# Gate and up products from seven half products, a feed-forward in two halves, adaLN weights in lots of four

## Chip, cores and metric

The kernel runs on one core of one Trainium2 chip. The metric is the device time of one execution in microseconds (us). TensorE (PE) multiplies, VectorE (DVE), ScalarE (ACT) and GpSimd (POOL) work elementwise, SyncE (SP) issues the loads. Before the change the median of three runs is 2294.38 us.

## What is computed

One inference step of a trunk of two layers, for a prompt of 512 tokens and 8 sequences with one new token each, 520 columns in all. Every layer has a feed-forward, a token mixer (gated delta rule beside windowed attention) and a second feed-forward. Each of them normalises its input, scales and shifts it by vectors made from a conditioning vector (adaLN), and adds its gated result to the residual stream. All in float32. The part that the change is about:

```python
def _adaln(c, w_ada, b_ada):
    m = jax.nn.silu(c) @ w_ada + b_ada
    return m.reshape(c.shape[0], N_MOD, 1, D_MODEL)      # 9 vectors of 1024

def _modulate(x, g, shift, scale):
    return _rms_norm(x, g) * (1.0 + scale) + shift

def _swiglu(h, w_gu, w_down):                            # w_gu (1024, 2 * 2816), w_down (2816, 1024)
    a, b = jnp.split(h @ w_gu, 2, axis=-1)
    return (jax.nn.silu(a) * b) @ w_down

def _layer(x, c, pos, conv_buf, S0, k_buf, v_buf, prm):
    ...
    m = _adaln(c, w_ada, b_ada)
    h = _modulate(x, g_ffn1, m[:, 0], m[:, 1])
    x = x + 0.5 * m[:, 2] * _swiglu(h, w_ffn1_gu, w_ffn1_down)
    h = _modulate(x, g_mix, m[:, 3], m[:, 4])
    ...
    x = x + m[:, 5] * mix
    h = _modulate(x, g_ffn2, m[:, 6], m[:, 7])
    x = x + 0.5 * m[:, 8] * _swiglu(h, w_ffn2_gu, w_ffn2_down)
```

## The kernel before

The residual stream `x` stays in SBUF with the 1024 features in 8 blocks of 128 partitions and the 520 tokens as columns. The columns are cut in two halves, a = 0 (256 columns) and a = 1 (264: 256 of the prompt and the 8 new tokens). Every product has a weight block of 128 by 128 as the stationary operand and up to 264 token columns as the moving one.

Float32 accuracy comes from three passes in a faster format: each operand is split into a rounded part and a rest (`whi` and `wlo` of the weights, `hh` and `hl` of the normalised input, `ghi` and `glo` of the gated values), and hh by whi, hl by whi and hh by wlo are summed in PSUM. `mmk` writes these three matmuls for one feature block k and one half, `mmk2` for both halves.

The class `Stream` (`W`) brings the weights: a `raw` tile of 1024 columns is loaded, cut in pieces of 512 columns (four blocks k), and each piece is split by one ACT copy (`whi`) and one DVE subtraction (`wlo`), into rings of eight buffers. `take` hands the next piece to the products; `advance` splits as many pieces ahead as the ring has room for, and is called after every block k.

A feed-forward (`ffn`) has 22 tiles of 128 hidden features. A tile needs a gate and an up product (`product`, 8 blocks k, 2 halves, 3 matmuls: 48 matmuls each), then `gate`: Silu on ACT, a product on DVE, and the split into `ghi` and `glo`. Tiles 0 and 1 are made by `head`, which goes over half a = 0 first, while half a = 1 is still being normalised by DVE and ACT (`Norm.apply`, one block k after the other; `norm.need` sets how far it must be). After the 22 tiles come 8 down products (22 blocks k each), whose results are added to `x` (`xupdate`); the last two of them are done half by half in `tail`, so that the normalisation of the next sub-layer can begin on half 0 while PE still works on half 1.

Work that is not in this line (the adaLN vectors, and most of the mixer) is in generators in a list (`Fill`). After every block k `fill.step` asks a clock model of the kernel's own whether a generator's next piece is ready, and writes its instructions there. `ada_gen` is one of these: for one adaLN vector it loads two groups of 8 weight tiles of 256 KB, and writes their 16 matmuls one after the other; four column groups of PE work on four of them at a time. Buffers for all this (`slot`) come from one pool of 48.

The stretch of the trace that is spoken of below, in order: feed-forward 1 of layer 0 to about 465 us, its mixer to about 777 us, feed-forward 2 of layer 0 to about 1198, feed-forward 1 of layer 1 to about 1595, the mixer, and feed-forward 2 of layer 1 from about 1907 us.

Of the kernel before, what the change touches and what calls it, by code (L numbers as in the profile page):

```python
# [25 lines left out]
SLOTS = 48  # L26
# [64 lines left out]
class Fill:  # L91
# [50 lines left out]

    def force(self):
# [15 lines left out]
class Stream:  # L159
# [3 lines left out]
    def __init__(self, ops, raw_p, hl_p, n_raw, n_sub):  # L163
        self.ops, self.raw_p, self.hl_p, self.n_raw, self.n_sub = ops, raw_p, hl_p, n_raw, n_sub
        self.descs, self.raw, self.subs = [], {}, []
        self.nd = 0
        self.free_raw = 0
        self.todo = []
        self.late = None
        self.out = 0  # L170

    def add(self, ap, keep=None):

        self.descs.append(ap)
        n = ap.shape[1]
        for o in range(0, n, 512):
            self.subs.append((len(self.descs) - 1, o, min(512, n - o), o + 512 >= n, keep))

    def advance(self, done, must=-1):
# [3 lines left out]
        while True:  # L183
# [9 lines left out]
            j = len(self.todo)  # L193
            if j < len(self.subs) and self.subs[j][0] < self.nd and self.room(done, j) and (
                    j <= must or clk.ready([self.raw[self.subs[j][0]]]) < clk.pe + 1.0):
                d, o, n, last, keep = self.subs[j]
                raw = self.raw[d]
# [14 lines left out]

    def rest(self):

        if self.late:
            j, d, lo, raw, hi = self.late
            self.late = None
            self.ops.tt(out=lo, in0=raw, in1=hi, op=ALU.subtract)
            if d is not None:
                del self.raw[d]  # L220
                self.free_raw = d + 1
# [17 lines left out]
class Ops:  # L239
# [22 lines left out]
    def mm(self, out, lhsT, rhs, start, stop, frac=1.0):  # L262
        self.nc.tensor.matmul(out, lhsT=lhsT, rhs=rhs, start=start, stop=stop)  # L263
# [73 lines left out]
def trunk(ctx, tc, xT, cT, cst, rope, vec, gu1, dn1, win, wba, wout, gu2, dn2, ada,  # L337
# [5 lines left out]
    raw_p = ctx.enter_context(tc.tile_pool(name="rawp", bufs=3))  # L343
# [8 lines left out]
    W = Stream(ops, raw_p, hl_p, 3, 8)  # L352

# [38 lines left out]
    hh = [(small(f"hh{a}", (128, KD, HALF[a][1]), F32R), small(f"hl{a}", (128, KD, HALF[a][1]), F32R)) for a in range(2)]  # L392
# [7 lines left out]
    def ada_load(l, g):  # L400
        t = []
        for k in range(KD):
# [5 lines left out]
    def ada_mm(t, pa, u=0, first=True, last=True):  # L408


        for k in range(KD):
            r = k % 4
            mm(pa[32 * r:32 * r + 32], lhsT=sc[:, u, k, :], rhs=t[k], start=first and k < 4, stop=last and k >= 4, frac=0.27)
# [17 lines left out]
    room = [True]  # L431
    mod_done = {(0, 0), (0, 1)}

    def ada_gen(l0):

        def load():
            if room[0] and mods and mods[0][0] <= l0:
                l, j = mods.pop(0)
                return l, j, ada_load(l, 2 * j), ada_load(l, 2 * j + 1)

        nxt = load()
        while nxt:
            l, j, t0, t1 = nxt
            yield t1
            pa = aux()
            ada_mm(t0, pa, 0, True, False)
            ada_mm(t1, pa, 1, False, True)
            m_sb = ada_out(pa)
            nxt = load()
            yield m_sb,  # L450
            ada_turn(l, 2 * j, m_sb, None, 2)
            mod_done.add((l, j))
# [87 lines left out]
    def mmk(out, w, k, src, kk, a, first, last, M=128):  # L540

        wh, wl = w
        for wi, (wt_, part) in enumerate(((wh, 0), (wh, 1), (wl, 0))):
            mm(out, lhsT=wt_[:, k * M:(k + 1) * M], rhs=src(a, part, kk), start=first and wi == 0, stop=last and wi == 2)
# [8 lines left out]
    def h_src(a, part, k):  # L553
        return hh[a][part][:, k, :]
# [24 lines left out]
    def head(norm):  # L579
# [18 lines left out]
        for k in range(KD):  # L598
            norm.need(1, k)
            for i in range(4):  # L600
                mmk(banks[1][i], ws[(k // 4) * 4 + i], k % 4, h_src, k, 1, k == 0, k == KD - 1)
            if k == 3:
# [81 lines left out]
    def ffn(l, j, norm, nxt, last, first=head):  # L684
        ghi, glo = [], []

        def gate(pg, pu):
# [7 lines left out]
            hi, lo = slot("ghi", F32R), slot("glo", F32R)  # L695
            act(out=hi, in_=t, func=AF.Copy)
            tt(out=lo, in0=t, in1=hi.bitcast(F32), op=ALU.subtract)
            ghi.append(hi)
            glo.append(lo)

        b = first(norm)
        gate(b[0], b[1])
        gate(b[2], b[3])
        for f in range(2, FF):
            room[0] = f < 12
            pg = product(h_src)
            pu = product(h_src)
            gate(pg, pu)

        def g_src(a, part, k):  # L710
            o, n = HALF[a]
            return (ghi, glo)[part][k][:, o:o + n]

        nrm = nxt() if nxt else None
        ops.table(EXP)
        for m in range(KD - 2):
            p = product(g_src, FF)
            for a in range(2):
                xupdate(l, j, m, p[a], a)
                if nrm is not None:  # L720
                    nrm.square(m, a)
            if last:
# [1042 lines left out]
```

## Time before, and how to read its profile

| what | value |
|---|---|
| median of three runs | 2294.38 us (2291.13 to 2298.29) |
| the profiled execution | 2294.32 us, of it 2292.5 us of span |
| PE busy | 2230.0 us (97%), 18154 matmuls |
| DVE busy | 1084.5 us (47%), 2586 instructions |
| ACT busy | 866.2 us (38%), 1861 instructions |
| POOL busy | 76.5 us (3%), 73 instructions |

Busy times are sums over the instructions of an engine. A matmul's own time in the trace (280 to 290 ns) is longer than the spacing at which matmuls follow each other (about 120 ns), since they overlap in the array; what a matmul costs is read from the spacing, that is from a stretch of the chain divided by its count. The same holds in a small way for DVE.

### The profile page before, as it was taken

The numbers are of one execution on the slowest core, as the hardware profiler recorded it, in microseconds if no ns is written. First come the engines' busy times: TensorE is split into PE (matmuls) and PEld (weight loads), VectorE is DVE, ScalarE is ACT, GpSimd is POOL, SyncE is SP. The second block draws the span as 40 slices with busy tenths as digits, with TensorE's granted clock in tenths as the row PEclk, the third lists the DMA queues.
The fourth block names the chain that finished last, engine by engine and source line by source line (L and its number), as shares of the span: only waits on it lengthen the run. The fifth ranks groups of instructions, "written<-read, shape, count | busy, mean of one in ns | idle before, by whom it ended". The sixth has DMA issues, their size and how long they took to land.

```text
span 2292.5 us, 43781 instructions
## 1 busy us (share of the span) xinstructions
PE 2230.0 (97%) x18154; PEld 2118.9 (92%) x18154; DVE 1084.5 (47%) x2586; ACT 866.2 (38%) x1861; POOL 76.5 (3%) x73
## 2 busy tenths in 40 slices
PE   7999999999988999999999999999998989999999
PEld 5879999989977988999999999999997879999999
DVE  5323333476787733333345333335687776333332
ACT  4323332356744422233234333323646444333321
POOL 0000000000121000000000000000001200000000
PEclk8999999999999999999999999999999999999999
DMA  8894223243224499422322222233432233222331
GB/s 270 317 325 148 93 86 95 91 96 104 84 66 130 170 326 337 155 93 86 95 88 93 93 92 93 85 95 101 88 103 63 77 134 120 92 89 89 94 113 52
DMA packets 172918, 287.75 MB, mean 126 GB/s; under 512 B 49936, under 2 KB 87472, under 8 KB 172720
## 3 DMA queue, kind: packets, MB, share of 16 engines
q1 hardware_dynamic: 172720, 284.96, 38.6%
q8 instruction: 142, 2.33, 0.4%
q14 instruction: 56, 0.46, 0.1%
HBM read 271.55 MB, written 14.41 MB: 125 GB/s over the span
## 4 chain that ended last, share of the span: by engine, by line
PE 85%; DVE 6%; issue 5%; ACT 3%; DMA 1%; POOL 0%; SPq 0%; DVEq 0%; POOLq 0%
PE acc L263 68%; PE aux L263 15%; DVE wlo L298 1%; DVE s L298 1%; PE aux L273 1%; ACT sq L290 1%; DVE hl L298 0%; DVE t L298 0%; DVE vr L298 0%; DVE w L298 0%; ACT whi L290 0%; POOL swa L307 0%; DVE ss L298 0%; DVE sq L298 0%; DVE x L298 0%
## 5 line engine op out<-in xcount | busy, mean ns | idle before, releaser
L263 PE MATMUL acc<-hh,whi 128*128 128x256 f32 x3440 | 742.1, 290 | 19.0 <-DVE x L298 12.3
L263 PE MATMUL acc<-hh,wlo 128*128 128x256 f32 x3440 | 721.1, 284 | 1.2 <-DVE wlo L298 1.2
L263 PE MATMUL acc<-hl,whi 128*128 128x256 f32 x3440 | 721.6, 284 | 0.0
L290 ACT ACTIVATE whi<-raw 128x512 fp32r<-128x512 f32 (+1 forms) x672 | 406.1, 617 | 751.4 <-PE acc L263 621.7
L298 DVE TENSOR_TENSOR wlo<-raw,whi 128x512 fp32r<-128x512 f32 (+1 forms) x672 | 437.4, 681 | 377.6 <-ACT whi L290 377.5
L263 PEld LDWEIGHTS acc<-hh,whi 128*128 128x128 f32 x3440 | 548.2, 189 | 58.0 <-issue 32.8
L263 PEld LDWEIGHTS acc<-hh,wlo 128*128 128x128 f32 x3440 | 546.1, 189 | 2.6 <-DVE wlo L298 2.6
L263 PEld LDWEIGHTS acc<-hl,whi 128*128 128x128 f32 x3440 | 547.3, 189 | 0.2
L263 PE MATMUL acc<-ghi,wlo 128*128 128x256 f32 x1232 | 262.0, 282 | 0.0
L263 PE MATMUL acc<-glo,whi 128*128 128x256 f32 x1232 | 261.7, 282 | 0.0
L263 PE MATMUL acc<-ghi,whi 128*128 128x256 f32 x1232 | 261.7, 282 | 0.0
L298 DVE TENSOR_TENSOR g<-g,acc 128x256 f32<-128x256 f32 (+1 forms) x168 | 64.2, 422 | 342.6 <-PE acc L263 306.0
L263 PEld LDWEIGHTS acc<-ghi,whi 128*128 128x128 f32 x1232 | 196.8, 188 | 0.0
L263 PEld LDWEIGHTS acc<-ghi,wlo 128*128 128x128 f32 x1232 | 196.6, 188 | 0.0
L263 PEld LDWEIGHTS acc<-glo,whi 128*128 128x128 f32 x1232 | 196.6, 188 | 0.0
L290 ACT ACTIVATE ghi<-g 128x520 fp32r<-128x520 f32 x88 | 56.2, 639 | 218.5 <-DVE g L298 218.5
L298 DVE SCALAR_TENSOR_TENSOR x<-acc,mt,x 128x256 f32<-128x256 f32 x72 | 33.6, 480 | 141.8 <-PE acc L263 141.8
L298 DVE TENSOR_TENSOR glo<-g,ghi 128x520 fp32r<-128x520 f32 x88 | 61.6, 701 | 62.2 <-ACT ghi L290 62.2
L263 PE MATMUL aux<-hl,whi 128*128 128x264 f32 x304 | 86.7, 285 | 0.8 <-DVE hl L298 0.8
L263 PE MATMUL aux<-hh,whi 128*128 128x264 f32 x304 | 86.9, 286 | 0.0
L263 PE MATMUL aux<-hh,wlo 128*128 128x264 f32 x304 | 86.4, 284 | 0.0
L263 PE MATMUL aux<-ada,sc 128*32 128x512 f32 (+1 forms) x640 | 71.6, 575 | 6.5 <-DMA ada<-in_ada 6.5
(289 smaller groups left out, 2145.1 us busy)
## 6 DMA issues: line engine op xcount, KB each, us to landing
raw<-in_gu SPq DMA_DIRECT2D x176, 512.0 KB, 3.2
ada<-in_ada SPq DMA_DIRECT2D x288, 256.0 KB, 5.4
raw<-in_dn SPq DMA_DIRECT2D x64, 512.0 KB, 3.5
raw<-in_win SPq DMA_DIRECT2D x44, 512.0 KB, 3.3
raw<-in_dn SPq DMA_DIRECT2D x32, 384.0 KB, 3.2
raw<-in_wout SPq DMA_DIRECT2D x22, 512.0 KB, 3.5
s<-in_s SPq DMA_DIRECT2D x16, 256.0 KB, 4.4
bv<-vnd SPq DMA_DIRECT2D x16, 256.0 KB, 4.3
```

The costliest lines, as they stand in the source:

```text
L263: self.nc.tensor.matmul(out, lhsT=lhsT, rhs=rhs, start=start, stop=stop)
L273: self.nc.tensor.transpose(out, in_, ident)
L290: self.nc.scalar.activation(**k)
L298: getattr(self.nc.vector, f)(**k)
```

## The change

The first matrix, h by the gate and up columns, is cut in two by two blocks: the tokens into the two halves a, the 1024 features into blocks k 0 to 3 and 4 to 7, and the columns of a tile into gate and up. The eight block products of a tile are replaced by seven (Strassen's scheme, in Winograd's form), for 78 of the 88 tiles: tiles 0 and 1 of each feed-forward, and in the first one tiles 2 and 3 too (`FIRST`), stay as they were.

- `add_pair` and `add_up`: for each such tile four sums of weight pieces are made on POOL (`sum`, 512 columns), and seven pieces are split in place of four.
- `combine`: once for a feed-forward, for each of four pairs of blocks k, POOL adds `hl` to `hh` again (four adds of 264 columns), DVE makes the four sums of the scheme from that (`y`), and ACT and DVE split them into four tiles `th`.
- `seven`: seven products of four blocks k, 12 matmuls each, five of them over 264 columns and two over 256. Three of them write on top of what another product left in the same PSUM bank, after ACT has copied it out (`u`); DVE adds the copies.
- The feed-forward is done in two halves of 11 tiles (`PARTS`), each followed by its 8 down products over 11 blocks k, so `x` is updated twice as often and each item of `tail` has 11 blocks k.
- `ada_gen` loads and multiplies lots of four tiles, four lots for an adaLN vector, as far as slots are free (`fits`), and writes them into PSUM buffers of the kind `acc` while the seven products run.
- 51 slots in place of 48, four `raw` tiles in place of three; `hh` and `hl` of half 0 are padded with zeros to 264 columns.

```diff
+    def add_pair(self, a0, a1):
+        d0, d1 = len(self.descs), len(self.descs) + 1
+        self.descs += [a0, a1]
+        a11, a12, a21, a22 = (("raw", d, o) for d in (d0, d1) for o in (0, 512))
+        j = len(self.subs)
+        s1, s2, s3, s4 = (("sum", j + i) for i in (3, 2, 4, 5))
+        self.sums += [(j + 2, s1, a21, a22, ALU.add, d1), (j + 2, s2, s1, a11, ALU.subtract, d1),
+                      (j + 4, s3, a11, a21, ALU.subtract, d1), (j + 5, s4, a12, s2, ALU.subtract, d1)]
+        self.uses.update({s1: 2, s2: 2, s3: 1, s4: 1})
+        for q in (a11, a12, s2, s1, s3, s4, a22):
+            self.subs.append((d1, q, 512, d1 if q == a22 else None, None))
...
+            t = self.made[q] = self.new_sum()
+            self.ops.pool("tensor_tensor", out=t, in0=self.source(x), in1=self.source(y), op=op)
...
-    def ada_mm(t, pa, u=0, first=True, last=True):
-        for k in range(KD):
-            r = k % 4
-            mm(pa[32 * r:32 * r + 32], lhsT=sc[:, u, k, :], rhs=t[k], start=first and k < 4, stop=last and k >= 4, frac=0.27)
+    def ada_mm(t, pa, u, h):
+        for r in range(4):
+            mm(pa[32 * r:32 * r + 32], lhsT=sc[:, u, 4 * h + r, :], rhs=t[r], start=u + h == 0, stop=u + h == 2, frac=0.27)
+        drop(*t)
...
+    def combine(norm, th):
+        for k in range(4):
+            yield lambda: norm.done[1] >= k + 5
+            h1, h2 = (slot("h32", F32, (128, 2, 264)) for _ in range(2))
+            for t, kk in ((h1, k), (h2, k + 4)):
+                for a in range(2):
+                    pool("tensor_tensor", out=t[:, a], in0=hh[a][0][:, kk, :].bitcast(F32),
+                         in1=hh[a][1][:, kk, :].bitcast(F32), op=ALU.add)
+            yield h1, h2
+            y0, y1 = (slot("y", F32, (128, 2, 264)) for _ in range(2))
+            tt(out=y0[:, 0], in0=h1[:, 1], in1=h1[:, 0], op=ALU.subtract)
+            tt(out=y1[:, 0], in0=h2[:, 1], in1=h1[:, 1], op=ALU.subtract)
+            tt(out=y0[:, 1], in0=h2[:, 1], in1=y0[:, 0], op=ALU.subtract)
+            tt(out=y1[:, 1], in0=h2[:, 0], in1=y0[:, 1], op=ALU.subtract)
...
+            act(out=x[0], in_=y0, func=AF.Copy)
+            act(out=x[2], in_=y1, func=AF.Copy)
+            yield y0, y1
+            tt(out=x[1], in0=y0, in1=x[0].bitcast(F32), op=ALU.subtract)
+            tt(out=x[3], in0=y1, in1=x[2].bitcast(F32), op=ALU.subtract)
...
+        def seven():
...
+            prod(pb, 264, of_h(0, 0, 264), True)
+            act(out=u1[:, 0], in_=pb[:, 0:264], func=AF.Copy)
+            prod(pa, 256, of_h(0, 4, 256), True)
+            tt(out=t0, in0=pa[:, 0:256], in1=u1[:, 0, 0:256], op=ALU.add)
+            prod(pb, 264, of_t(0, 1), False)
+            act(out=u1[:, 1], in_=pb[:, 0:264], func=AF.Copy)
+            act(out=t0, in_=t0, func=AF.Silu)
+            prod(pc, 264, of_t(0, 0), True)
+            act(out=u2[:, 1], in_=pc[:, 0:264], func=AF.Copy)
+            prod(pb, 264, of_t(2, 0), False)
+            act(out=u2[:, 0], in_=pb[:, 0:264], func=AF.Copy)
+            prod(pc, 264, of_h(1, 4, 264), False)
+            tt(out=t1, in0=pc[:, 0:264], in1=u1[:, 1], op=ALU.add)
+            tt(out=u2[:, 1], in0=u2[:, 1], in1=u2[:, 0], op=ALU.add)
+            prod(pb, 256, of_t(2, 1, 256), False)
...
+        for part, (f0, f1) in enumerate(PARTS):
+            nk = f1 - f0
+            for f in range(max(f0, 2), f1):
...
+                fill.until(lambda: len(th) == 4)
+                pairs[0] = True
+                seven()
```

What the change does to the order of the instructions, at three places.

DVE, the instructions of one tile in the middle of a feed-forward, and the first of the next, before (`g` is the gated tile, `acc` its PSUM):

```order
L298 TENSOR_TENSOR wlo<-raw,whi 128x512 x4
L298 TENSOR_TENSOR g<-g,acc 128x256
L298 TENSOR_TENSOR g<-g,acc 128x264
L298 TENSOR_TENSOR glo<-g,ghi 128x520
L298 TENSOR_TENSOR wlo<-raw,whi 128x512 x3
```

and after (`sum` comes from POOL, `u` are the copies out of PSUM, `aux` and `acc` are PSUM):

```order
L352 TENSOR_TENSOR wlo<-raw,whi 128x512
L352 TENSOR_TENSOR glo<-g,ghi 128x520
L352 TENSOR_TENSOR wlo<-sum,whi 128x512 x3
L352 TENSOR_TENSOR g<-aux,u 128x264
L352 TENSOR_TENSOR u<-u 128x264
L352 TENSOR_TENSOR wlo<-sum,whi 128x512
L352 TENSOR_TENSOR g<-g,aux 128x256
L352 TENSOR_TENSOR wlo<-raw,whi 128x512
L352 TENSOR_TENSOR g<-g,u 128x264
L352 TENSOR_TENSOR wlo<-raw,whi 128x512
L352 TENSOR_TENSOR g<-acc,u 128x256
```

From 7 instructions a tile it has become 13, of which three read PSUM and ten have both inputs in SBUF.

DVE again, at the head of feed-forward 2 of layer 0, from the normalisation of half 1 on (`hl_77` is the rest part of half 1, one row for a block k), before:

```order
L298 SCALAR_TENSOR_TENSOR hl_77<-ss,mt_80,hh_76 128x256
L298 SCALAR_TENSOR_TENSOR ss<-x,mt_80,rs 128x256
L298 TENSOR_TENSOR wlo<-raw,whi 128x512 x3
L298 SCALAR_TENSOR_TENSOR hl_77<-sq,mt_80,hh_76 128x256
L298 SCALAR_TENSOR_TENSOR hl_77<-ss,mt_80,hh_76 128x256
L298 TENSOR_TENSOR g<-g,acc 128x256
```

and after (`h_9512` and so on are the sums that POOL makes for `combine`):

```order
L352 SCALAR_TENSOR_TENSOR hl_77<-ss,mt_80,hh_76 128x256
L352 SCALAR_TENSOR_TENSOR ss<-x,mt_80,rs 128x256
L352 TENSOR_TENSOR y<-h_9512 128x264
L352 TENSOR_TENSOR y<-h_9513,h_9512 128x264
L352 TENSOR_TENSOR y<-h_9513,y 128x264 x2
L352 TENSOR_TENSOR th<-y,th 128x528 x2
L352 TENSOR_TENSOR wlo<-raw,whi 128x512 x2
L352 TENSOR_TENSOR wlo<-sum,whi 128x512
L352 TENSOR_TENSOR y<-h_9599 128x264
L352 TENSOR_TENSOR y<-h_9600,h_9599 128x264
L352 TENSOR_TENSOR y<-h_9600,y 128x264 x2
L352 SCALAR_TENSOR_TENSOR hl_77<-sq,mt_80,hh_76 128x256
```

The last two blocks of `hl_77` now stand behind the first two and three of the four rounds of `combine`; the last pair of `th` comes behind the gates of tiles 0 and 1.

PE, an adaLN vector among gate and up products, before:

```order
L263 MATMUL acc<-hh_74,wlo 128x256
L263 MATMUL acc<-hh_76,wlo 128x264
L263 MATMUL aux<-ada,sc 32x512 x16
L263 MATMUL acc<-hh_74,whi 128x256
L263 MATMUL acc<-hh_76,whi 128x264
```

and after, one of its four lots, which stands in the middle of a half product:

```order
L317 MATMUL aux<-hl_77,whi 128x264
L317 MATMUL aux<-hh_76,wlo 128x264
L317 MATMUL acc<-ada,sc 32x512 x4
L317 MATMUL aux<-hh_76,whi 128x264
L317 MATMUL aux<-hl_77,whi 128x264
```

16 matmuls in one run have become four runs of four at different places; the sixteen vectors that `ada_gen` makes have 64 such runs.

## Rows read from the trace of the kernel before

**Rows 1.** The page: engines busy us; granted clock of PE in 40 slices.

```profile
PE 2230.0 (97%) x18154; PEld 2118.9 (92%) x18154; DVE 1084.5 (47%) x2586; ACT 866.2 (38%) x1861; POOL 76.5 (3%) x73
...
PEclk8999999999999999999999999999999999999999
```

**Rows 2.** Windows: layer 1, feed-forward 1 (first line: columns).

```profile
core 0: us, PE busy (x) PEld busy (x) DVE busy (x) ACT busy (x) POOL busy (x), PEclk, DMA share, GB/s
1206.00:1558.00 352.00, 351.75 (x2916) 351.54 (x2917) 126.83 (x244) 110.30 (x212) 0.00 (x0) 1.00 0.28 91
```

**Rows 3.** Chain that ended last: start us, us, what; 264 columns, 256, both.

```profile
1173.76 8.05 PE aux L263 x66
1181.81 7.78 PE acc L263 x66
...
1222.83 334.82 PE acc L263 x2778
```

**Rows 4.** Groups by line: shapes xcount, busy us, mean ns, idle before it.

```profile
L298 DVE TENSOR_TENSOR wlo<-raw,whi 128x512 fp32r<-128x512 f32 (+1 forms) x672 | 437.4, 681 | 377.6 <-ACT whi L290 377.5
L290 ACT ACTIVATE whi<-raw 128x512 fp32r<-128x512 f32 (+1 forms) x672 | 406.1, 617 | 751.4 <-PE acc L263 621.7 <-PE aux L263 56.9 <-ACT whi L290 44.0
...
L298 DVE TENSOR_TENSOR g<-g,acc 128x256 f32<-128x256 f32 (+1 forms) x168 | 64.2, 422 | 342.6 <-PE acc L263 306.0 <-ACT g L290 31.5 <-issue 3.9
```

**Rows 5.** Timeline of DVE, 651 to 660 us: start us, us, instruction.

```profile
651.68 0.69 DVE L298 TENSOR_TENSOR X<-X,aux 128x512 f32<-128x512 f32 x1 [2.42 <-PE aux L263]
652.28 2.88 DVE L298 TENSOR_TENSOR klo<-raw,khi 128x512 fp32r<-128x512 f32 x2
655.08 2.96 DVE L298 TENSOR_TENSOR wlo<-raw,whi 128x512 fp32r<-128x512 f32 x3
657.96 0.68 DVE L298 TENSOR_TENSOR X<-X,aux 128x512 f32<-128x512 f32 x1
658.56 0.67 DVE L298 TENSOR_TENSOR XT<-XT,aux 128x512 f32<-128x512 f32 x1
```

**Rows 6.** Timeline of POOL, the same stretch and two others.

```profile
649.20 7.09 POOL L307 TENSOR_TENSOR mb<-B,cs 128x512 f32<-128x512 f32 x5 [13.54 <-PE aux L263]
...
608.63 2.52 POOL L307 TENSOR_TENSOR mb<-B,cs 128x512 f32<-128x512 f32 x2 [10.76 <-DMA out_convs<-cs]
...
692.05 4.04 POOL L307 TENSOR_TENSOR s<-s,bc 128x512 f32<-128x512 f32 x4 [10.80 <-PE aux L263]
```

**Rows 7.** Timeline of PE around one adaLN vector.

```profile
164.73 0.40 PE L263 MATMUL acc<-hh,wlo 128*128 128x256 f32 x2
165.06 3.64 PE L263 MATMUL aux<-ada,sc 128*32 128x512 f32 x32
168.63 0.51 PE L263 MATMUL acc<-hh,whi 128*128 128x256 f32 x2
168.98 0.28 PE L263 MATMUL acc<-hl,whi 128*128 128x256 f32 x1
```

**Rows 8.** Chain, head of layer 0's feed-forward 2, half 1.

```profile
789.71 11.75 PE aux L263 x96
```

**Rows 9.** Timeline of DVE, same place, hl of half 1.

```profile
787.53 0.48 DVE L298 SCALAR_TENSOR_TENSOR hl<-sq,mt,hh 128x256 fp32r<-128x256 f32 x1 [0.18 <-ACT hh L290]
...
791.21 0.48 DVE L298 SCALAR_TENSOR_TENSOR hl<-sq,mt,hh 128x256 fp32r<-128x256 f32 x1
```

**Rows 10.** Chain, end of layer 0's feed-forward 2 into the next head.

```profile
1189.58 2.65 PE aux L263 x20
...
1205.21 0.61 DVE wlo L298
...
1205.87 4.21 PE acc L263 x33
```

**Rows 11.** Windows, after a gap of PE in the mixer of layer 0.

```profile
643.80:650.60 6.80, 3.59 (x17) 3.62 (x18) 5.23 (x11) 0.60 (x1) 1.40 (x2) 0.50 0.38 79
```

**Rows 12.** Timeline of PE just before that window.

```profile
647.01 1.83 PE L263 MATMUL aux<-XT,mb 128*128 128x128 f32 x7 [5.60 <-DVE XT L298]
```

More of the change, by code (lines that the diff above doesn't have):

```diff
@@ L141, in step, with try_ @@
         return True
+    def try_(self, e):
+        if e in self.q and e[0] <= self.clk.pe + 0.05 and (e[2] is None or e[2]()):
+            self.run(e)
     def force(self):
@@ L211, in advance, with there @@
                 return
+    def there(self, j):
+        d, q = self.subs[j][:2]
+        if q[0] == "sum" and q not in self.made:
+            return 1e9
+        return self.ops.clk.ready([self.raw[d] if q[0] == "raw" else self.made[q]])
     def rest(self):
         if self.late:
-            j, d, lo, raw, hi = self.late
+            j, q, last, lo, src, hi = self.late
             self.late = None
[L218 to L221, printed above, removed]
+            self.ops.tt(out=lo, in0=src, in1=hi, op=ALU.subtract)
+            self.used(q)
+            if last is not None:
+                self.free_raw = last + 1
     def room(self, done, j):
@@ L537, in apply, with mmk @@
                             yield ()
[L540 removed]
+    def mmk(out, w, k, src, kk, a, first, last, M=128, join=False):
         wh, wl = w
         for wi, (wt_, part) in enumerate(((wh, 0), (wh, 1), (wl, 0))):
[L544 removed]
+            mm(out, lhsT=wt_[:, k * M:(k + 1) * M], rhs=src(a, part, kk), start=first and wi == 0, stop=last and wi == 2,
+               join=join)
     def mmk2(ac, w, k, src, kk, first, last, M=128):
@@ L694, in gate, with of_h, of_t, prod @@
                 tt(out=t[:, o:o + n], in0=t[:, o:o + n], in1=pu[a], op=ALU.mult)
[L695 to L701, printed above, removed]
+            for f in split(t):
+                f()
+        unit = []
+        def seven():
+            pb, pc = aux(), aux()
+            if not unit:
+                u = acc()
+                unit.extend((u[:, 0], u[:, 1]))
+            pa = unit.pop(0)
+            t = slot("g")
+            u1, u2 = (slot("u", F32, (128, 2, 264)) for _ in range(2))
+            t0, t1 = t[:, 0:256], t[:, 256:520]
+            def of_h(a, k0, n):
+                return lambda _, part, k: hh[a][part][:, k0 + k, 0:n]
+            def of_t(i, c, n=264):
+                return lambda _, part, k: th[k][i + part][:, c, 0:n]
+            def prod(bank, n, src, first):
+                w = W.take()
+                for k in range(4):
+                    mmk(bank[:, 0:n], w, k, src, k, 0, first and k == 0, k == 3, join=not first)
+                    W.advance(W.out - 1)
+                    fill.step()
+                go()
+            prod(pb, 264, of_h(0, 0, 264), True)
[13 more added lines that the diff above has]
+            prod(pb, 256, of_t(2, 1, 256), False)
+            act(out=t1, in_=t1, func=AF.Silu)
+            tt(out=t0, in0=t0, in1=pb[:, 0:256], op=ALU.mult)
+            def end():
+                tt(out=t1, in0=t1, in1=u2[:, 1], op=ALU.mult)
+                drop(u1, u2)
+            later(end, *split(t))
@@ L702, in ffn @@
+        sums = {t.tensor.name for t in W.made.values()}
+        if first is None:
+            used.intersection_update(sums)
+            used.update(q.tensor.name for q in (norm.ss, *norm.sqs, norm.rs) if q is not None)
+            e = fill.add(combine(norm, th), 0.5)
+            fill.run(e)
+            b = head(norm, e)
+        else:
+            b = first(norm)
+            used.intersection_update(sums)
+            e = fill.add(combine(norm, th), 0.5)
         gate(b[0], b[1])
         gate(b[2], b[3])
[L704 to L722, printed above, removed]
-                dma(out=y_o[:, m], in_=x[:, m])
-        y, z = KD - 2, KD - 1
-        items = [(0, y, True, True, True), (1, y, False, False, True), (0, z, True, True, True), (1, z, False, False, True)]
```

208 lines of the change are left out of this document (155 added, 53 removed).

## The prediction

> **What bounds the kernel now.** I read the page first: PE is busy 97% of the span, and its clock is granted at full speed in nearly every slice [rows 1]. A feed-forward then shows as one stretch in which PE is busy in 351.75 of 352 us, while DVE has work for 126.83 and POOL for none [rows 2]. The chain that ended last says the same: 2778 matmuls in 334.82 us, 0.1205 us each, with nothing between them [rows 3]. So a feed-forward costs what its matmuls cost, and a matmul fewer is time saved, as long as DVE, ACT and POOL keep up. The other two rows of that group give the two shapes: 8.05 / 66 = 0.1220 us for 264 columns, 7.78 / 66 = 0.1179 us for 256.
>
> **Term 1, the matmuls: -106.5 us.** A tile has 48 matmuls of either shape: 48 x 0.1179 + 48 x 0.1220 = 11.52 us. Seven half products have 84, 24 of them narrow: 24 x 0.1179 + 60 x 0.1220 = 10.15 us. That is 1.365 us a tile; 88 tiles less the 10 plain ones make 78, so 106.5 us. The down products keep their count, and every matmul loads its own weights now [rows 1], so that is not lost. The loads from memory keep their bytes, in 32 pieces more for the down weights, on a queue that PE does not wait for in a feed-forward [rows 2]. This gain comes whole only if nothing else is the slowest in a tile.
>
> **Term 2, DVE with POOL in a tile: +8 us.** DVE instructions overlap a little: three of 512 columns start 0.60 apart though each lasts 0.68 [rows 5]. I therefore take 0.60 for `wlo`, 0.61 for `glo`, and 0.422 - 0.08 = 0.34 for those of 256 or 264 columns [rows 4]. Before, a tile is 4 x 0.60 + 2 x 0.34 + 0.61 = 3.7 us of DVE; after, 7 x 0.60 + 5 x 0.34 + 0.61 = 6.5 us, still under 10.15. But POOL, idle until now, gets four adds of 512 columns. Their price has two nearest rows: 4.04 / 4 = 1.01 us and 2.52 / 2 = 1.26 us [rows 6]; the middle is 1.13, so 4.5 us a tile. And the two engines hinder each other: at 652.28 two DVE instructions with both inputs in SBUF took 2.88 us and the next three 2.96, 5.76 us up to 658.04, where five spaced by 0.60 and the last one's tail make 3.1 [rows 5]; POOL was at work until 656.29 [rows 6]. In these 4.0 us DVE lost 2.7. The instruction just before, which reads PSUM, took its ordinary 0.69 under the same POOL work.
>
> The Trainium skill, "SBUF — State Buffer", section "Who interferes with whom", states this as a rule: VectorE's second read port is also GpSimd's, and an instruction with two SBUF inputs and a GpSimd instruction that reads SBUF shut each other out for their whole length. The trace agrees, with 2.88 us against 1.28 for a free pair. Taken without any overlap the rule gives a tile of 6.5 + 4.5 = 11.0 us and the whole about 2292; without the rule this term is nothing, and the whole 2246.
>
> From the rows alone: ten of the 13 DVE instructions of a tile read only SBUF, three (1.0 us) read PSUM and can run under POOL. DVE needs between 6.5 + 4.0 - 1.0 = 9.5 and 6.5 + 5.0 = 11.5 us; I take the middle, 10.5, which is 0.35 more than PE's 10.15. Not all of it reaches PE: the rings of eight pieces let splitting run about seven half products ahead, and the copies out of PSUM have one half product (1.45 us) to spare, so some 2.5 us of lag are absorbed in a part, and the down products behind it let DVE recover. Eight parts with 78 tiles: 78 x 0.35 - 8 x 2.5 = 7.3, say 8 us. Bounds: 0, and at 11.5 us 78 x 1.4 - 20 = 89.
>
> ACT has 7 `whi` of 0.617 us [rows 4] and seven instructions that I bound by the same: at most 8.6 us a tile. It stays hidden, behind PE.
>
> **Term 3, combine: +30 us.** Before the first seven-product tile, `th` must be there. It starts when block 4 of half 1 is normalised. In feed-forward 2 of layer 0 this is 791.21 + 0.48 = 791.7 [rows 9], and half 1 of tiles 0 and 1 runs from 789.71 to 801.46 [rows 8]. Behind it PE has one adaLN lot (0.9, a quarter of 3.57 from rows 7) and two half products that need no `th` (24 x 0.12 = 2.9), and it asks for the last pair of `th` some 1.1 later: 806.4. What must be done by then: 16 POOL adds of 264 columns, at 0.58 (half of 1.13 and a little), 9.3 us, and two `sum` of 1.13; on DVE, from the order at that place, 16 `y` of 0.34, 8 splits `th` of 0.62, three `wlo`, two `hl` of 0.40, two `glo`: 14.3 us. All of these read SBUF alone, so by the lock that rows 5 show they go one after the other: 25.8 us, to 817.5. PE waits 11 us, part of it already for `hl` of blocks 6 and 7, which now stand behind `y`. I take 10. Without the lock DVE's own 14.3 would end it near 807.5: 1 to 2 us. Three heads have this (both feed-forwards 2 and the first of layer 1): 30, between 5 and 39. In the first feed-forward tiles 2 and 3 give PE 23 us more, and I count nothing.
>
> **Term 4, the tails: +12 us.** The last item of `tail` (half 1) covers the normalisation of half 0 for the next head. At the end of feed-forward 2 of layer 0 the chain leaves PE at 1192.23, goes through ACT and DVE and comes back to PE at 1205.87, released by DVE [rows 10]: the cover is just used up. With 11 blocks k in place of 22 it is 33 x 0.122 = 4.0 us shorter. Three tails have a head behind them: 12 us; 6 if the lighter work beside it speeds the chain.
>
> **Term 5, adaLN lots: +9.6 us.** A run of adaLN matmuls starts 0.09 late (165.06 against 164.73 + 0.24) and the two matmuls behind it take 0.35 in place of 0.24 [rows 7]: 0.2 us a run. 64 runs in place of 16 make 48 more. The same loads are spread over more time; nothing is counted for that.
>
> **Term 6, the clock: +7 us.** After a gap of 5.60 us [rows 12] the granted clock was 0.50 for 6.8 us [rows 11], the 1.2 GHz level. Each of the three heads will have longer gaps; at half speed such a stretch costs up to 3.4 us. I take 7 for the three, between 0 and 10.
>
> Sum: -106.5 + 8 + 30 + 12 + 9.6 + 7 = -39.9. The profiled execution took 2294.32, the median of three is 2294.38, so one base serves both: **2254 us**.
>
> **The rivals.**
> - *Clean.* DVE and POOL fit beside PE after all, combine costs 5, tails 6, the clock nothing: -106.5 + 5 + 6 + 9.6 = -86, 2208 us. For it: DVE and ACT now idle more than half the span [rows 1]. Against: the DVE rows under POOL [rows 5].
> - *DVE with POOL bounds the tile: slower.* With POOL adds at 1.26 and nothing run beneath them a tile takes 11.5 us, hardly less than 11.52: 2294.3 - 106.5 + 89 + 30 + 12 + 9.6 + 7 = 2335. It decides where 78 x - 20 (x: excess over 10.15) passes 106.5 - 58.6 = 47.9, at x = 0.87, a tile of 11.0 us. For it: those five instructions lost 2.7 of 4.0 us. Against: three reads of PSUM a tile go free, and POOL's work may fall where DVE waits for PE anyhow.
> - *The shared banks make PE wait: no change.* Products 3, 5, 6 and 7 write into a bank that ACT or DVE must have read. ACT's copy stands behind a Silu, which waits for a DVE add that stands behind `wlo`. If that costs 0.6 us a tile, it is 47 in place of 8: 2293. Against: a whole half product lies between the read and the next write.
>
> **How the numbers follow.** Chances: forecast 0.56, clean 0.17, slower 0.17, shared banks 0.10. The likeliest one's own range is 2225 to 2285, from its terms' bounds. For 8 in 10 I go down below the clean case and up past no change to a tile near 11.1 us: 2198 to 2316. A difference of 0.3% is about 7 us here and about what a measurement of this kernel can tell from none: faster has the forecast, clean and a little of the third, 0.76; same 0.07; slower 0.17.
>
> **What the profile of the changed kernel would show.** Term 1: some 936 matmuls fewer, and 84 to a tile of about 10.2 to 10.6 us. Term 2: DVE busy far more than 6.5 us a tile, `wlo` with a mean well above 681 ns, POOL adds above 1.13. Term 3: gaps of PE of about 10 us in three heads, released by DVE `hl` or `th`. Term 4: gaps of some 4 us behind three tails. Term 5: 64 runs of eight, 0.2 us lost at each. Term 6: half clock after those gaps. I would be wrong if PE stands still in every tile (second and third rival), or if the heads show no gap.

## The result, and the profile after

The changed kernel takes 2312.99 us (median of four runs, 2309.65 to 2314.33) against 2295.42 for the kernel before in the same comparison: a ratio of 1.0076 with a 95% interval of 1.0056 to 1.0096. It is slower by 0.8%; the prediction said 1.8% faster. The profiled execution took 2309.65 us, 2307.9 of it span.

The page of the changed kernel, its busy times and the granted clock, answers to [rows 1]:

```profile
PE 2158.9 (94%) x17218; PEld 2018.2 (87%) x17218; DVE 1657.3 (72%) x3278; ACT 1116.8 (48%) x2438; POOL 627.4 (27%) x451
...
PEclk8999999999999989999997999999999998999999
```

There are 936 matmuls fewer, as forecast, and PE is busy 71.1 us less. But the span is 15.4 us longer, so PE now stands still some 86 us more. The 7 and the two 8s within the row of the clock are new as well. Where PE stands still is said by PE's waits over the whole span: what it waited for, us in all, times, the longest.

```profile
PE aux L317 <- DVE hl L352: 32.0, 6, 8.5
PE aux L317 <- ACT g L344: 17.7, 3, 5.9
...
PE aux L327 <- ACT ada_sb L344: 8.0, 2, 7.3
PE acc L317 <- DVE t L352: 7.9, 7, 1.1
```

The first two, 49.7 us, are three gaps in each of the three heads that the prediction spoke of; the other two lie in the first feed-forward but for 0.7 us of `ada_sb` ahead of it, and of that feed-forward the prediction expected nothing. The windows of layer 1's feed-forward 1 (answering to [rows 2]), of eleven of its tiles, and of the head of layer 0's feed-forward 2; columns as there:

```profile
1206.00:1568.00 362.00, 341.16 (x2754) 336.23 (x2754) 279.44 (x434) 181.01 (x375) 138.75 (x95) 0.97 0.30 91
1414.30:1528.20 113.90, 113.15 (x927) 111.71 (x927) 103.32 (x144) 71.05 (x153) 57.77 (x37) 1.00 0.33 102
806.90:830.80 23.90, 10.27 (x43) 7.99 (x44) 21.41 (x29) 9.21 (x19) 12.75 (x11) 0.50 0.07 23
```

The tiles are sound: 113.90 / 11 = 10.35 us each, and PE stands still for 0.75 us in eleven of them. The head is not: from within its first gap on, the granted clock is at half (1.2 GHz) for 23.90 us, and the 10.27 us that PE works in this stretch are 5.1 us more than at full clock.

**What happens in that head.** PE's timeline there, its three gaps in brackets:

```profile
812.31 0.59 PE L317 MATMUL aux<-hl,whi 128*128 128x264 f32 x1 [8.46 <-DVE hl L352]
...
817.65 0.59 PE L317 MATMUL aux<-hl,whi 128*128 128x264 f32 x1 [2.33 <-DVE hl L352]
...
826.33 1.94 PE L317 MATMUL aux<-ada,sc 128*32 128x512 f32 x8 [5.89 <-ACT g L344]
```

DVE's timeline (start, us):

```profile
805.60 2.41 DVE L352 TENSOR_TENSOR th<-y,th 128x528 fp32r<-128x528 f32 x2
807.93 1.83 DVE L352 TENSOR_TENSOR wlo<-raw,whi 128x512 fp32r<-128x512 f32 x2
...
810.29 0.42 DVE L352 TENSOR_TENSOR y<-h 128x264 f32<-128x264 f32 x1
810.63 0.42 DVE L352 TENSOR_TENSOR y<-h,h 128x264 f32<-128x264 f32 x1
...
811.78 0.48 DVE L352 SCALAR_TENSOR_TENSOR hl<-sq,mt,hh 128x256 fp32r<-128x256 f32 x1
...
813.98 0.97 DVE L352 TENSOR_TENSOR y<-h 128x264 f32<-128x264 f32 x1
814.87 0.97 DVE L352 TENSOR_TENSOR y<-h,h 128x264 f32<-128x264 f32 x1
...
817.12 0.48 DVE L352 SCALAR_TENSOR_TENSOR hl<-ss,mt,hh 128x256 fp32r<-128x256 f32 x1
...
819.30 1.50 DVE L352 TENSOR_TENSOR y<-h 128x264 f32<-128x264 f32 x1
820.73 1.49 DVE L352 TENSOR_TENSOR y<-h,h 128x264 f32<-128x264 f32 x1
822.14 2.91 DVE L352 TENSOR_TENSOR y<-h,y 128x264 f32<-128x264 f32 x2
```

POOL's, the adds `h` of combine and the sums of the next pair:

```profile
801.76 6.85 POOL L361 TENSOR_TENSOR h<-hh,hl 128x264 f32<-128x264 f32 x7
812.40 4.04 POOL L361 TENSOR_TENSOR h<-hh,hl 128x264 f32<-128x264 f32 x4 [3.79 <-DVE hl L352]
...
818.78 1.74 POOL L361 TENSOR_TENSOR sum<-raw 128x512 f32<-128x512 f32 x1
820.59 1.33 POOL L361 TENSOR_TENSOR sum<-sum,raw 128x512 f32<-128x512 f32 x1
```

and ACT's:

```profile
823.66 0.64 ACT L344 ACTIVATE th<-y 128x528 fp32r<-128x528 f32 x1 [5.71 <-DVE y L352]
825.09 0.64 ACT L344 ACTIVATE th<-y 128x528 fp32r<-128x528 f32 x1 [0.79 <-DVE y L352]
825.63 0.37 ACT L344 ACTIVATE g<-acc 128x256 f32<-128x256 f32 x1
825.90 0.38 ACT L344 ACTIVATE g<-aux 128x264 f32<-128x264 f32 x1
```

Read the four together. While POOL is idle (808.61 to 812.40) a `y` takes 0.42 us and the next starts 0.34 later. Beside POOL's `h` adds it takes 0.97 and the next starts 0.89 later; beside a sum, 1.50 and 1.43. The instruction `hl` that PE waits for stands between them in DVE's queue: each of the first two gaps ends as the `hl` of block 6 or 7 ends (812.26, 817.60). The third has another path: the last `y` end at 825.05, ACT's copies `th` wait for them, the Silu `g` of tile 0 stands behind the copies, and the bank that it reads is the one that PE wants next. PE starts as ACT has read it. The other two heads repeat this: 8.46 + 2.33 + 5.89 = 16.7, then 16.3 and 16.8 us.

### The profile page after: what moved, and what is told of

It reads as the page before. It is cut to its first block, busy times and chain, and to the rows that moved or that the text cites. A ratio compares the mean times of both kernels' runs of the same rounds, so it can differ in the third digit from the quotient of the medians.

```text
span 2307.9 us, 44270 instructions
## 1 busy us (share of the span) xinstructions
PE 2158.9 (94%) x17218; PEld 2018.2 (87%) x17218; DVE 1657.3 (72%) x3278; ACT 1116.8 (48%) x2438; POOL 627.4 (27%) x451
## 4 chain that ended last, share of the span: by engine, by line
PE 79%; DVE 13%; ACT 4%; issue 2%; DMA 1%; SPq 0%; POOL 0%; DVEq 0%; ACTq 0%
PE aux L317 40%; PE acc L317 38%; DVE y L352 2%; DVE wlo L352 2%; DVE hl L352 1%; DVE sq L352 1%; ACT whi L344 1%; PE aux L327 1%; DVE th L352 1%; DVE ss L352 1%; ACT sq L344 1%; DVE g L352 1%; ACT s L344 1%; DVE s L352 1%; DVE x L352 1%
## 5 line engine op out<-in xcount | busy, mean ns | idle before, releaser
L361 POOL TENSOR_TENSOR sum<-raw 128x512 f32<-128x512 f32 x156 | 247.2, 1585 | 848.3 <-DMA raw<-in_gu 664.1
L317 PE MATMUL aux<-th,whi 128*128 128x264 f32 (+1 forms) x2496 | 467.5, 286 | 3.7 <-ACT u L344 3.6
L317 PEld LDWEIGHTS aux<-th,whi 128*128 128x128 f32 x2496 | 384.8, 188 | 27.3 <-issue 13.4
L317 PE MATMUL aux<-th,wlo 128*128 128x264 f32 (+1 forms) x1248 | 353.3, 283 | 0.0
L352 DVE TENSOR_TENSOR wlo<-sum,whi 128x512 fp32r<-128x512 f32 x312 | 335.3, 1106 | 19.0 <-ACT whi L344 16.6
L317 PE MATMUL acc<-hh,whi 128*128 128x256 f32 x1256 | 326.0, 301 | 19.0 <-DVE x L352 14.7
L317 PE MATMUL acc<-hl,whi 128*128 128x256 f32 x1256 | 306.3, 285 | 6.7 <-DVE hl L352 6.3
L317 PE MATMUL acc<-hh,wlo 128*128 128x256 f32 x1256 | 305.9, 285 | 6.7 <-DVE wlo L352 6.7
L317 PE MATMUL aux<-hh,whi 128*128 128x264 f32 x928 | 273.0, 294 | 11.8 <-ACT g L344 11.8
L317 PEld LDWEIGHTS acc<-hh,whi 128*128 128x128 f32 x1256 | 220.3, 192 | 54.5 <-issue 37.0
L317 PEld LDWEIGHTS acc<-hl,whi 128*128 128x128 f32 x1256 | 219.3, 192 | 8.3 <-DVE hl L352 7.9
L317 PEld LDWEIGHTS acc<-hh,wlo 128*128 128x128 f32 x1256 | 219.2, 191 | 8.1 <-DVE wlo L352 8.0
```

What stands on the lines that cost most here:

```text
L352: getattr(self.nc.vector, f)(**k)
L361: getattr(self.nc.gpsimd, f)(**k)
```

## The experiments

The theory after the result (A): the matmuls saved what they should; the loss lies in the heads, where VectorE and GpSimd shut each other out and the instructions that PE needs stand behind combine's in the queues of DVE and ACT; and in the tails, the lots and the clock. The rivals: the loss lies in the tiles, in the cut into halves and lots, or in the length of DVE's own work. The kernel before took 2295.66, 2294.81 and 2295.02 us in the three groups (e1 to e4, e5 to e8, e9 to e12). Behind each measured time stands its ratio to the kernel before, with the 95% interval; a head's gaps are those above 0.6 us unless another bound is named.

**e1_no_combine.** Combine's work is left out: the seven products read `hh` and `hl` in place of `th`. The number of buffers that must stay free before a lot is loaded is raised by the sixteen that `th` no longer takes.

```diff
-            return len(used) + 4 <= SLOTS - 13
+            return len(used) + 4 <= SLOTS - 29
...
-                return lambda _, part, k: th[k][i + part][:, c, 0:n]
+                return lambda _, part, k: hh[c][part][:, 2 * i + k, 0:n]
...
-            e = fill.add(combine(norm, th), 0.5)
-            fill.run(e)
-            b = head(norm, e)
+            b = head(norm)
...
```

> Leaves out combine: the seven products read hh and hl themselves, so no h, y or th is made and the result is another; matmuls, weight sums, lots and halves stay. Theory A (the loss sits in the heads, where combine's chain of DVE and POOL and the half clock behind it hold PE up; the tiles give what was forecast): the three head gaps (16.7, 16.3, 16.8 us), some 15 us of half clock and about 10 us in the first feed-forward go, 2313 - 75 = 2238, between 2228 and 2252. Theory B (the tiles themselves do not gain, because DVE and POOL bound them): only the heads' gaps go while tiles stay slow, 2265 or more.

Measured 2258.94 us, 0.9840 [0.9825, 0.9854]: 54 us below the changed kernel, but 21 above what theory A expected, between the ranges of the two theories. Combine is the largest single cost. Of the 21 us some 10 are gaps that stay in the heads (3.3, 2.7 and 4.1 us, gaps above 0.15 us counted), and 8 are seven gaps of 1.13 us in the first part of layer 0's feed-forward 2, which the changed kernel does not have there; its own seven, in the first feed-forward, stay as well (below).

**e2_no_sums.** The sums are left out: the pieces that were sums are split from `raw`.

```diff
-        for q in (a11, a12, s2, s1, s3, s4, a22):
-            self.subs.append((d1, q, 512, d1 if q == a22 else None, None))
+        for i, q in enumerate((a11, a12, a21, a11, a12, a21, a22)):
+            self.subs.append((d1, q, 512, d1 if i == 6 else None, None))
...
```

> Leaves out the POOL sums of weights: the seven pieces of a tile are split from raw columns (three of them twice), so the result is another; combine keeps its POOL adds. Theory A: a tile goes from 10.33 to about 10.2 us (-10 us in all), and in the heads the y of the last round are no longer held up by sums (4 to 6 us in each of three): 2313 - 25 = 2288, between 2275 and 2300. Theory B (sharing of DVE and POOL in the tiles is the loss): -60 us, 2250.

Measured 2278.76, 0.9922 [0.9907, 0.9937], in theory A's range. The third gap of a head fell from 5.9 to 1.79 us and the first to between 4.8 and 6.4. The gap of 7.3 us in the first feed-forward is gone too, and the seven of 1.13 us stand in layer 0's feed-forward 2 instead. Its window of eleven seven-product tiles:

```profile
1397.90:1509.20 111.30, 111.30 (x927) 111.30 (x926) 76.00 (x144) 71.86 (x153) 0.00 (x0) 1.00 0.35 104
```

**e3_all_plain.** All tiles plain, without combine and sums; the halves and the lots as in the change, the bound on free buffers as in e1.

```diff
-FIRST = 4
+FIRST = 22
...
-    def ffn(l, j, norm, nxt, last, first=None, plain=2):
+    def ffn(l, j, norm, nxt, last, first=None, plain=22):
...
```

> Same result as the reference's, but no tile uses seven products (all 22 plain, no combine, no sums); the halves of 11 tiles and the adaLN lots of four stay. Theory A with the forecast's terms 4 and 5: shorter cover in three tails 12 us, 48 more runs of adaLN matmuls 9.6 us, some half clock behind the tails 3 us: 2295 + 25 = 2320. Rival (halves and lots cost nothing, all of the loss is in the seven products): 2295.

Measured 2323.85, 1.0123 [1.0108, 1.0139]: the halves, the lots and what goes with them cost 28 us, as theory A has it (2320). Eleven plain tiles, the same stretch:

```profile
1412.00:1538.90 126.90, 126.90 (x1058) 126.90 (x1058) 43.14 (x78) 38.98 (x76) 0.00 (x0) 1.00 0.27 86
```

(126.90 - 111.30) / 11 = 1.42 us a tile is what seven half products save when nothing hinders them. In the changed kernel the same eleven take 113.90: the sums cost 0.24 us a tile there.

**e4_norm_first.** Combine begins only when all of half 1 is normalised.

```diff
-            yield lambda: norm.done[1] >= k + 5
+            yield lambda: norm.done[1] >= 8
```

> combine starts only when all 8 blocks of half 1 are normalised, in place of block 4; nothing else is changed. Theory A (the chain of combine as a whole is what PE waits for): the two gaps before hl go (8.5 and 2.3 us in each head) but the wait for th grows by as much or more, 2313, between 2303 and 2325. Rival C (what costs is that hl of blocks 6 and 7 stand behind y): 3 x 10.8 us less, 2281.

Measured 2300.70, 1.0025 [1.0015, 1.0035], outside both: 2 us below theory A's range and 20 above rival C. In layer 1 the waiting moved rather than went: what stands before `hl` shrank to 0.7 and 2.5 us, 2.1 and 1.3 stand before a bank that `g` frees, and 13.7 before the first product that reads `th` (ended by ACT's copy `u`), 16.6 and 17.5 us for the two heads in place of 16.3 and 16.8. The head of layer 0 fell to 9.5; why that one alone is open.

**e5_plain4.** Tiles 2 and 3 plain in every feed-forward.

```diff
-    def ffn(l, j, norm, nxt, last, first=None, plain=2):
+    def ffn(l, j, norm, nxt, last, first=None, plain=4):
...
```

> Tiles 2 and 3 are plain (16 half products) in all four feed-forwards instead of the first alone, so the products th that combine makes are wanted some 23 us later. Six tiles more are plain: 6 x 1.365 = +8.2 us. Theory A (the gaps of a head have two causes: hl of blocks 6 and 7, which stand behind combine's adds and subtractions, and only the third gap waits for th): the third gap (5.9 us) goes from three heads, 17.7 us, the first two (8.3 and 2.3) stay, so with the half clock that follows 2300 to 2306 us. Rival B (all of a head's waiting is for th): 50 us of gaps and 15 of half clock go, 2313 + 8 - 65 = 2256.

Measured 2307.15, 1.0056 [1.0041, 1.0071], 1 us above theory A's range and far from rival B. PE's waits:

```profile
PE aux L317 <- DVE hl L352: 25.5, 6, 6.3
...
PE acc L317 <- DVE g L352: 7.1, 3, 3.2
```

Later use of `th` alone does not free the head, since two of its three gaps are not about `th`: 5.9 to 6.3 and 2.3 us before `hl` stay. The third did not go wholly: 2.0, 2.0 and 3.2 us stand before a bank that the gate of a tile frees. And layer 0's feed-forward 2 has seven gaps of 1.13 us, as in e1.

**e6_tail_order.** Two down products of half 1 behind the last of half 0.

```diff
-                items = [(0, y, ...), (1, y, ...), (0, z, ...), (1, z, ...)]
+                items = [(0, y, ...), (0, z, ...), (1, y, ...), (1, z, ...)]
```

> The four last down products of a tail run as half 0 of y, half 0 of z, half 1 of y, half 1 of z, so that two products of half 1 (8 us) cover the normalisation of half 0. Theory A (the tail's cover became 4 us too short in each of three tails, with a stretch at half clock behind two): 13.2 + 3.4 us go, 2296 us (2292 to 2301). Rival B (the head's first matmuls wait for a chain that starts only with the last product): within 5 us of the changed kernel, 2308 to 2315.

Measured 2301.22, 1.0030 [1.0018, 1.0042]: 11.8 us below the changed kernel, where 16 were to be had, and 0.2 above theory A's range. The gaps behind the tails are gone but for one of 2.11 us and two of 0.7; four gaps of 0.7 us inside the tails are new.

**e7_no_pool.** The sums and combine's adds on VectorE.

```diff
-            self.ops.pool("tensor_tensor", out=t, in0=self.source(x), in1=self.source(y), op=op)
+            self.ops.tt(out=t, in0=self.source(x), in1=self.source(y), op=op)
...
-                    pool("tensor_tensor", out=t[:, a], in0=hh[a][0][:, kk, :].bitcast(F32),
+                    tt(out=t[:, a], in0=hh[a][0][:, kk, :].bitcast(F32),
```

> The four sums of a pair and the sixteen adds of combine run on VectorE instead of GpSimd; nothing else changes, and GpSimd is idle in a feed-forward. Theory A (a VectorE instruction with two SBUF inputs and a GpSimd add shut each other out, so that moving the adds to VectorE costs VectorE less than it frees): VectorE needs 6.5 + 4 x 0.6 = 8.9 us a tile, the tile goes from 10.34 to 10.15 us (-15), combine's chain is shorter by some 4 us in three heads, and the first feed-forward's gap of 7.3 shrinks: 2285 us (2270 to 2298). Rival B (the two engines run side by side and VectorE's own queue is what is late): VectorE gets 16 x 0.34 + 4 x 0.6 = 7.8 us more in each head, 2313 + 24 = 2337, or more where the tile suffers.

Measured 2272.48, 0.9905 [0.9891, 0.9920]: 40.5 us below the changed kernel, at the fast end of theory A's range. Groups by line of the changed kernel, with the mean ns of one behind the busy time,

```profile
L352 DVE TENSOR_TENSOR wlo<-sum,whi 128x512 fp32r<-128x512 f32 x312 | 335.3, 1106 | 19.0 <-ACT whi L344 16.6 <-PE acc L317 2.3
...
L361 POOL TENSOR_TENSOR sum<-raw 128x512 f32<-128x512 f32 x156 | 247.2, 1585 | 848.3 <-DMA raw<-in_gu 664.1 <-DVE wlo L352 65.2 <-PE acc L317 37.8
```

and of e7:

```profile
L352 DVE TENSOR_TENSOR wlo<-sum,whi 128x512 fp32r<-128x512 f32 x312 | 203.7, 683 | 19.0 <-ACT whi L344 18.8
L352 DVE TENSOR_TENSOR sum<-raw 128x512 f32<-128x512 f32 x156 | 106.5, 683 | 0.5 <-DMA raw<-in_gu 0.5
```

and e7's window of eleven tiles:

```profile
1382.10:1493.50 111.40, 111.40 (x928) 111.40 (x927) 96.48 (x182) 72.96 (x153) 0.00 (x0) 1.00 0.34 104
```

A `wlo` of a sum is back at 683 ns (681 for all `wlo` in [rows 4]). With 376 instructions more, DVE is busy less: 1589.3 us on e7's page in place of 1657.3. In the eleven tiles it needs 96.48 us where it needed 103.32 beside POOL, and the tile is 10.13 us. The heads fell less, to 8.3, 12.6 and 14.7 us. What is left there is mostly combine on DVE's own queue, since without combine (e1) a head has 2.7 to 4.1 us. Some 11 us come from the first feed-forward: its seven gaps of 1.13 us are gone, and the one of 7.3 is 2.4, with a new one of 2.0.

**e8_all.** e4, e5, e6 and e7 together.

> All together: tiles 2 and 3 plain everywhere, the tail in the order half 0, half 0, half 1, half 1, no work on GpSimd, and combine beginning only when all blocks of half 1 are normalised. Theory A (the time of the changed kernel above the sum of its matmuls is what stands at the heads, tails and in the tile, each for the reason named): of 2313 go some 42 of head gaps, 12 of half clock, 16 at tails, 15 in tiles, and 8 come for six plain tiles: 2236 us (2225 to 2260), ahead of both kernels. Rival B (the parts take the same waiting from one another, because what is removed at one place is waited for at the next): 2270 or more.

Measured 2255.02, 0.9823 [0.9807, 0.9839], inside theory A's range, at its upper end. Its heads have 1.2, 8.1 and 8.0 us of gaps, and the seven of 1.13 us stand in layer 0's feed-forward 2.

**e9_open_lot.** e8, and a lower bound on free buffers for lots during the down products of a first part.

```diff
-            return len(used) + 4 <= SLOTS - 13
+            return len(used) + 4 <= SLOTS - (4 if downs[0] else 13)
...
```

> The version with all four repairs, and during the down products of a feed-forward's first part an adaLN lot may load whenever four slots are free (13 were kept free), so that a vector opened in the tiles is finished and gives its accumulator bank back. Theory A (in that version seven gaps of 1.13 us stand before the down products 920 to 976 us, because the open vector holds one of two accumulators): 7.9 us go, 2247 us (2243 to 2252). Rival B (what the lots then cost in the down products eats it): 2255.

Measured 2238.09, 0.9760 [0.9742, 0.9777]: 17 us below e8, 5 us below theory A's range. The seven gaps of 1.13 us are gone; so they were what the theory says. The other 9 us were not forecast. Lots that ran among tiles now run in the down products. PE works 12.5 us less at half clock (45.6 in place of 58.1), but 11.0 of these lie in the two mixers, which the edit does not touch; that this part comes from the edit is not shown.

**e10_all_but_nf.** e8 without e4's edit.

> The version with all repairs, but combine begins block by block again, as in the change. Theory A (with tiles 2 and 3 plain combine has time enough, and its instructions only delay hl, for which PE waits some 5 us in three heads): 2255 + 8 to 15 with the half clock behind such gaps, 2266 us (2261 to 2272). Rival B (starting early is what lets combine finish before tile 4; the gap of 2.5 us at th, twice, and the one of 4.2 go): 2246 us.

Measured 2238.19, 0.9753 [0.9736, 0.9770]: 17 us below e8, and 8 below what rival B said; theory A is refuted. Once tiles 2 and 3 are plain and POOL is out of the way, starting combine early does no harm. Of gaps above 1 us two heads have one each, of 3.74 and 3.32 us before `hl`, the third two (3.78 and 1.19). The seven gaps of 1.13 us are absent here too; they are 7.9 of the 17 us, and the gaps of the heads came down by only some 3. The rest was not traced to the order of combine.

**e11_combine_dve, e12_sums_dve.** One half of e7's edit each: combine's adds, or the sums, on VectorE.

> The changed kernel with combine's 16 adds on VectorE, the sums of a pair still on GpSimd. Theory A (exclusion of the two engines; it acts in the head through combine's adds and in the tile through the sums): the head is shorter, as in the run with nothing on GpSimd (its gaps 37 us in place of 50, half of the saving of clock), but the tile stays at 10.34: about 2295 us (2287 to 2303). Rival B (the whole gain of that run came from the sums, which stand ahead of combine's adds on GpSimd): 2313 or more.

> The changed kernel with the four sums of a pair on VectorE, combine's adds still on GpSimd. Theory A: the tile goes from 10.34 to 10.15 us (some 12 to 15 us in all), the third gap of a head from 5.9 to about 2 as without sums (12 us), the first two gaps stay: 2286 us (2280 to 2296). Rival B (sums on VectorE cost there what they free): 2310.

Measured 2286.66 (0.9966 [0.9954, 0.9979]) and 2281.26 (0.9942 [0.9927, 0.9957]). Both halves help, and the tile gains by the sums alone. e12 does what was expected: the tile is 10.13 us, and the three heads have 37.5 us of gaps, against 35.6 in e7; the third gap of a head is 1.8 us, as in e2:

```profile
PE aux L317 <- ACT g L344: 5.4, 3, 1.8
```

e11 came out 0.3 us below theory A's range, and partly in another place than expected: layer 0's head fell to 8.4 us, but layer 1's stayed at 16.5 and 17.1, with most of the waiting now before the first product that reads `th`; 12.7 us came from the first feed-forward, whose gaps went or shrank. They did so in e12 too, which is part of why the two savings, 26 and 32 us, add up to more than e7's 40.5.

## Why the prediction was wrong

The working below lays PE's rows over the granted clock: PE was idle 58.9 us up to its last matmul before, 144.9 after (+86.0). It was busy 2230.0 before, 32.8 of it at half clock; 2158.9 after, 79.3 of it at half clock.

**Term 1, the matmuls (-106.5): right.** Busy time with the half-clock part counted at full speed is 2220.3 us in e3 and 2113.3 in e2: -107.0.

**Term 2, the tile (+8): the right kind, and if anything too small.** 10.35 us with POOL against 10.12 without; if all 78 tiles lose as much, that is 18. Busy time at full clock leaves 6 for it against e2 (2119.3 - 2113.3) and 12 against e7 (2119.3 - 2107.5), with some 2 to 4 of short gaps. So it is between 8 and 18. POOL's price was too low: a sum took 1.5 to 1.6 us in the place of 1.13. But those microseconds contain the waiting for DVE, and so don't add to DVE's. The rival that DVE with POOL bounds the tile would have needed 11.0 us. The shared banks (third rival; four products of a tile write on top of another's result, not three as the list of the change has it) cost at most 0.75 / 11 = 0.07 us a tile.

**Term 3, combine (+30, at most 39): the step that failed, 49.7 us.** Its prices and its rule held: `y` and `h` take turns, 0.89 us for the two, and I had added 0.34 + 0.58. The Trainium skill's rule that the prediction gave ("SBUF — State Buffer", "Who interferes with whom") agrees with that and with e7. What failed is the queue that I drew. I laid the work end to end from 791.7 to 817.5 and let PE wait once, at `th`. In the trace it ran from 793.4 to 831.5, with one add of half 0 ahead of that. Six sums fell in that time, two counted; POOL stood idle for `hl` between blocks (3.1 and 3.8 us), so the two queues also waited for one another in turn; and the cover that I credited behind the head (an adaLN lot, two half products) came too late, because PE stood still inside the head: first at `hl`, which I had named and counted as a part of the same wait, and then at a bank held by a Silu behind ACT's `th` copies, which I had named only for the tiles. e5 shows the first (the gaps at `hl` stay when `th` is not wanted), e2 and e12 the second (5.9 to 1.8 us without sums on POOL).

**Term 4, the tails (+12): right, 13.2.** Two of the six gaps, answering to [rows 10]:

```profile
464.07 0.39 PE L317 MATMUL acc<-hh,wlo 128*128 128x256 f32 x1 [3.76 <-DVE wlo L352]
```

```profile
1214.66 0.38 PE L317 MATMUL acc<-hl,whi 128*128 128x256 f32 x1 [2.40 <-DVE hl L352]
```

**Term 5, the lots (+9.6): somewhat too large, 6.7.** A lot among the matmuls of a tile, PE's timeline, answering to [rows 7]:

```profile
272.04 0.28 PE L317 MATMUL aux<-hh,wlo 128*128 128x264 f32 x1
272.26 1.06 PE L317 MATMUL acc<-ada,sc 128*32 128x512 f32 x8
273.25 0.39 PE L317 MATMUL aux<-hh,whi 128*128 128x264 f32 x1
273.48 0.29 PE L317 MATMUL aux<-hl,whi 128*128 128x264 f32 x1
```

It starts 0.10 late, and the next two matmuls are 0.23 apart where 0.12 is usual: 0.2 us. e3 has 6.7 us more busy time than before at full clock, for 48 lots more.

**Term 6, the clock (+7, at most 10): too small; 23 us measured.** (79.3 - 32.8) / 2 = 23.2 us in the whole kernel, 15 of it in the three heads. I took one stretch of 6.8 us [rows 11] as the length of such a fall; behind three gaps in a row it was 23.90.

**What the sum did not have: the first feed-forward, 15 us.** I counted nothing there, since tiles 2 and 3 cover combine. They cover `th`, but not PE's other work: an adaLN vector's copy `ada_sb` stands behind the same `th` copies on ACT. PE's timeline, and ACT's:

```profile
94.85 1.11 PE L327 MATMUL aux<-cs,ada_sb 128*128 128x128 f32 x4 [7.31 <-ACT ada_sb L344]
```

```profile
91.80 0.64 ACT L344 ACTIVATE th<-y 128x528 fp32r<-128x528 f32 x1 [1.70 <-DVE y L352]
93.15 0.64 ACT L344 ACTIVATE th<-y 128x528 fp32r<-128x528 f32 x1 [0.71 <-DVE y L352]
...
94.22 0.58 ACT L344 ACTIVATE ada_sb<-aux 128x512 f32<-128x512 f32 x1
```

And a vector that was opened in the tiles keeps one of the two `acc` buffers through the down products, when too few buffers are free for its next lot: here the first lot of the fifth vector runs at 154.34 and the second at 268.54, with the down products between. They use one buffer in turn and wait for `x` to be updated, seven times 1.13 us:

```profile
154.34 1.06 PE L317 MATMUL acc<-ada,sc 128*32 128x512 f32 x8
...
196.04 0.48 PE L317 MATMUL acc<-ghi,whi 128*128 128x256 f32 x2 [1.13 <-DVE t L352]
...
268.54 1.41 PE L317 MATMUL acc<-ada,sc 128*32 128x512 f32 x8
```

e9 shows this cause by removing it, for the same seven gaps where e8 has them, in layer 0's feed-forward 2. I had written that the same loads are spread over more time and counted nothing for it.

Together: -107.0 + 12.7 (lots and tile in busy time) + 23.2 (clock) gives the -71.1 of busy time; 49.7 + 13.2 + 15.2 and 7.9 of small ones (the largest some 3 us more in each mixer, in e3 too; their cause was not looked for) give the 86.0 of idle time. The difference is +14.9, against -39.9 forecast: 20 from combine, 16 from the clock, 15 from the first feed-forward, the rest from small terms. That 2313 lies within the wide range (2198 to 2316) is luck: its upper end stood for a tile of 11.1 us that DVE with POOL bound, and the tile is 10.35.

The change pays 1% with the adds off POOL alone (e7), and more when tiles 2 and 3 are plain and the tails have their old cover too. e10's page, answering to the one above:

```profile
PE 2148.3 (96%) x17290; PEld 2016.9 (90%) x17290; DVE 1555.7 (70%) x3594; ACT 1103.1 (49%) x2396; POOL 79.2 (4%) x75
...
PEclk8999999999999999999999999999999989999999
```

e9 and e10 are both faster than either kernel, by 2.4% than the one before. The two were not combined.

## What to carry to other kernels

Where a producer of operands runs on the engines that also free the consumer's banks and make its other operands, don't place one end time: walk each in-order queue and ask what stands behind every new instruction, since the wait comes at the first of those, not at the new result. Moving elementwise work to an idle GpSimd is not free when VectorE reads two SBUF operands at that time; here VectorE was busy less with the work than beside it. Products that save matmuls lose them again where PE pauses, and then once more, since the granted clock fell to half around these pauses.

## What was not expected of the hardware

Three gaps of 8.5, 2.3 and 5.9 us within 23 us kept the granted clock at 0.50 for 23.90 us in each of three heads, where one gap of 5.60 had cost 6.80 us at that level. The Trainium skill ("GPSIMD Engine Reference", "4.1 Engine selection") advises VectorE for elementwise work on a tile and calls GpSimd about twice as slow with two inputs; the runs agree and go further: a sum took 1585 ns on GpSimd beside VectorE's work (the waiting for VectorE included) and 683 on VectorE, and its move also brought VectorE's own `wlo` of these pieces from 1106 to 683 ns.
